# Rotary keys of four tiles at once, transposes inside projections, and a later start of the last query latents

## The chip, the cores and the metric

The kernel runs on one core of a Trainium2 chip. The metric is the device time of one execution in microseconds (us). TensorE, below also PE, does the matrix products and the transposes; VectorE (DVE), ScalarE (ACT) and GpSimd (POOL) do the rest, of which GpSimd works on SBUF alone; SP issues most DMAs.

## The reference

One layer of a bidirectional encoder for 1024 tokens and 16 learned meta tokens of width 1024, in float32. After an RMS norm one projection feeds two kinds of attention: multi-head latent attention (8 heads, queries and keys rebuilt from latents of 256) and neighbourhood attention (16 heads on a grid of 16 by 64 tokens). Each result is multiplied with a SiLU gate; an output projection and the residual follow. The part that matters here:

```python
q_nope, q_pe = split(rmsnorm(q_lat) @ w_uq)        # 128 + 64 per head
k_nope, v    = split(rmsnorm(kv_lat) @ w_ukv)      # 128 + 128 per head
q = [rmsnorm(q_nope), rope(rmsnorm(q_pe))]         # positions 0 to 1039
k = [rmsnorm(k_nope), rope(rmsnorm(k_pe))]         # k_pe: one rotary key for all heads
o = softmax(q k^T / sqrt(192)) v
```

## The kernel before

Products of float32 are made of three matmuls on rounded parts, high times high, low times high and high times low; so a value that TensorE will read is evicted twice, a high part (often by ScalarE) and a low part, the difference (often by VectorE: `lo_of`, L114). Weights are loaded into `wnf` and split by casts into `wnh` (L160) and `wnl`.

The stages are: gates, the neighbourhood attention (a pipelined loop over `g`, whose last six steps fill TensorE with projections of key-value latents), the rest of the latents, the latent attention (a loop over steps `s`, head `h` and query tile `t` of 128 rows, eight tiles a head), and the output projection. On TensorE the instructions stand in the order in which the code issues them, and it runs them in that order. On the other engines a scheduler puts them in order by its own estimate of time, and each engine then keeps that order.

The latents: there are eight tiles of 128 tokens and a ninth, number 8 (`NT`), of the 16 meta tokens. For each, `proj` makes the key-value latent and the raw rotary key (320 columns, 24 matmuls, for the meta tile 16), `lat_nat` takes squares on ScalarE, makes the inverse root mean square (`rstd`, a chain of small instructions with a power on GpSimd) and scales (`natl`), `lat_rope` rotates the key of a tile, and `lat_tr` transposes latent and key and evicts them (`klT`, `KH`, `KL`). `order` is the order of these tiles. Then come the same for the q latents (256 columns, `qlT`), and among them head 0's key-value tiles: `kv_tile` (6 matmuls of 256 columns, normalization of the keys, values into `mV`) and two steps later `kv_tr` (transposes into `mkT`). `q_tile` makes a query tile of a head pair (6 matmuls of 384 columns, `mqraw`, `mqr` the rotated part) and two steps later `q_tr` transposes it into `mq`.

In a step of the latent attention TensorE does the scores of the tile in three blocks of columns (`m_qk`, 348, 346 and 346 columns, 5 matmuls each), and with them the transposes of the probabilities of the step before (`m_ptr`), the products with the values (`m_pv`), and the tiles of the next head by the list `kv_now` and `q_now`. What a step has put into `pend` is transposed two steps later. In before, head 0's query tile `s+4` is made in step `s`, transposed in step `s+2` and used in step `s+4`.

Of the kernel before, what the change touches and what calls it, by code (L numbers as in the profile page):

```python
# [49 lines left out]
def hybrid_layer(ctx, tc, x, x_t, meta, meta_t, norm_w, w_na, w_g, w_lat, lat_w, w_uq, w_ukv, vec128, qpe_w, kpe_w,  # L50
# [634 lines left out]
    def lat_nat(t, acc, q, sq, pieces=None, late=None):

        n = P if t < NT else NM
        k = 1 if q else 2
# [13 lines left out]
        if pieces:  # L702
            nats[q, t] = pieces
            for k_, pc in enumerate(pieces):
                V.tensor_scalar(pc, acc[:, k_ * P:(k_ + 1) * P], r[:, 0:1], None, op0=ALU.mult)
            return
# [165 lines left out]
    def lat_rope(t):  # L872
        n = P if t < NT else NM
        kr = mk.tile([P, P], F32, name="kr", tag="mkn", bufs=6)[:n]
        rope(kr.rearrange("p (h k d) -> p h k d", h=1, k=2), nats.pop(("pe", t)).rearrange("p (h d) -> p h d", h=1),
             tabk[:n, t], n, 1, mk, V)
        nats["r", t] = kr

    def lat_tr(t, q, bank):
        n = P if t < NT else NM  # L880
        kc = k0 = slice(t * P, t * P + n)
        ps = bank("tr").rearrange("p (k n) -> p k n", k=4)[:, :, :n]
        nat = nats.pop((q, t))
        for k in range(2):
            tr(ps[:, k, :], nat[k])
        if not q:
            tr(ps[:, 2, :], nats.pop(("r", t)))
# [22 lines left out]
    for t in order[:3]:  # L910
        lat_rope(t)
    for i in range(LEAD, NT + 1):
        t = order[i]
# [3 lines left out]
        for k in ((0, 1), (2, 3, 4), (5, 6))[i - LEAD]:
            lat_tr(order[k], False, bank)
        for k in ((3, 4), (5, 6), (7,))[i - LEAD]:
            lat_rope(order[k])  # L920
    lat_rope(order[NT])
# [41 lines left out]
    for i in range(NT):  # L963
        acc = bank("o" if i % 2 else "s")[:, :256]
        proj(acc, i, wq, 0, 256)
        lat_nat(i, acc, True, lat_sq(), None if i < NT - 1 else
                [mk.tile([P, P], F32, name="natq", tag="mkn", bufs=6) for _ in range(2)])
# [6 lines left out]
        if i < 2:  # L974
            lat_tr(order[NT - 1 + i], False, bank)
        else:
            lat_tr(i - 2, True, bank)
        for ts_ in (((), (), (0, 1), (2, 3), (4,), (5,), (6,), (7, 8))[i],):
# [383 lines left out]
```

## Time and profile before

| | |
|---|---|
| median of 3 runs | 1341.32 us (1341.28 to 1343.41) |
| profiled execution | 1344.79 us, span 1343.0 us |
| granted TensorE clock over the span | 0.992 |
| latents, from the end of the neighbourhood attention | 672.75 to 739.79 us |
| latent attention, head 0 (eight steps) | 739.79 to 794.76 us |
| heads 1 to 7 | from 794.76 us, to about 1150 |

A step's start is the first matmul of its scores (`mps_s<-mkT,mq`, 348 columns). In a timeline an instruction stands with start, duration and, in brackets, the idle time of its engine ahead of it and what ended it. Consecutive matmuls overlap in the timeline, so the distance of two starts tells the pace and not the duration.

### The profile page before, as it was taken

To read this page: it belongs to the slowest core of one execution; us is meant where nothing else is said; L and a number is where in the kernel's file an instruction comes from. 1 tells how busy PE (TensorE), PEld (TensorE's weight loads), DVE (VectorE), ACT (ScalarE), POOL (GpSimd) and SP (SyncE) were. 2 spreads that over 40 slices of the span, in tenths; PEclk is the share of its full clock that TensorE was granted. 3 is DMA by queue.
4 is the path that set the end of the run, shared out by engine and by line. 5 is a ranking of instruction groups with operands and counts; after the bars stand their busy time and mean duration, and the time that the engine had idled before them with its cause. 6 is when DMAs were issued, how large, how long until landed. Compare 5 with 4: busy or idle time off the path is not lost.

```text
span 1343.0 us, 24641 instructions
## 1 busy us (share of the span) xinstructions
PE 1301.1 (97%) x8116; PEld 1202.7 (90%) x8116; DVE 956.9 (71%) x3100; ACT 806.5 (60%) x2263; POOL 398.2 (30%) x851
## 2 busy tenths in 40 slices
PE   9999999999999999999987999999999999999999
PEld 7888889999999999998987989999999999988887
DVE  4933236898988988888778889988988998542110
ACT  6622135787777878777755767777777786531010
POOL 4422102212122112212345437526625751000000
PEclk9999999999999999999999999999999999999999
DMA  9352640131212222111121010000100122353231
GB/s 340 134 175 82 213 140 27 52 102 49 76 42 79 79 70 71 45 57 51 44 60 52 13 37 23 33 27 24 34 32 17 48 80 75 87 173 118 81 96 47
DMA packets 82254, 103.59 MB, mean 77 GB/s; under 512 B 10311, under 2 KB 60871, under 8 KB 82007
## 3 DMA queue, kind: packets, MB, share of 16 engines
q1 hardware_dynamic: 82127, 102.02, 24.2%
q8 instruction: 64, 1.05, 0.3%
q14 instruction: 63, 0.52, 0.1%
HBM read 70.80 MB, written 24.90 MB: 71 GB/s over the span
## 4 chain that ended last, share of the span: by engine, by line
PE 61%; DVE 20%; ACT 11%; issue 4%; DMA 2%; POOL 1%; SPq 0%; ACTq 0%; DVEq 0%; POOLq 0%
PE ps_acc L117 14%; PE mps_acc L117 10%; PE mps_s L117 8%; PE ps_s L117 8%; PE mps_st L117 7%; PE mps_o L117 5%; PE mps_tr L120 4%; PE ps_o L117 3%; ACT s_sb L592 2%; DVE qs L557 2%; ACT qz L554 2%; PE ps_tr L120 2%; DVE s_sb L587 2%; DVE PT L114 2%; DVE m_sb L1034 2%
## 5 line engine op out<-in xcount | busy, mean ns | idle before, releaser
L93 POOL TENSOR_TENSOR rs_y<-rs_v,mhalf 128x1 f32<-128x1 f32 (+5 forms) x170 | 149.4, 882 | 84.0 <-DVE rs_v L89 61.3
L117 PE MATMUL ps_acc<-wnh,hT 128*128 128x384 f32 (+1 forms) x432 | 159.5, 369 | 0.0
L117 PE MATMUL ps_acc<-wnh,hTl 128*128 128x384 f32 (+1 forms) x432 | 144.6, 335 | 0.0
L117 PE MATMUL ps_acc<-wnl,hT 128*128 128x384 f32 (+1 forms) x432 | 144.1, 334 | 0.0
L558 POOL CAST qs<-qz 64x128 fp32r<-64x128 f32 x128 | 38.3, 299 | 339.5 <-ACT qz L554 327.1
L117 PE MATMUL mps_s<-mkT,mq 128*128 128x346 f32 (+1 forms) x576 | 132.3, 338 | 1.3 <-DVE mPT L114 0.9
L1060 ACT CAST mPT<-mps_tr 128x512 fp32r<-128x512 f32 x128 | 74.4, 583 | 54.5 <-PE mps_tr L120 53.4
L117 PE MATMUL mps_o<-mPT,mV 128*128 128x256 f32 x768 | 106.2, 287 | 0.0
L1034 DVE TENSOR_SCALAR_CACHE_REDUCE m_sb<-mps_s 128x346 f32<-128x346 f32 (+1 forms) x192 | 97.4, 513 | 10.0 <-PE mps_s L117 8.0
L592 ACT ACTIVATE s_sb<-s_sb,nmn 128x400 f32<-128x400 f32 (+1 forms) x128 | 76.7, 600 | 38.7 <-DVE nmn L587 38.3
L114 DVE TENSOR_TENSOR mPT<-mps_tr,mPT 128x512 fp32r<-128x512 f32 x128 | 87.7, 686 | 13.4 <-ACT mPT L1060 12.2
L117 PEld LDWEIGHTS mps_s<-mkT,mq 128*128 128x128 f32 x576 | 93.4, 192 | 3.2 <-DVE mPT L114 1.5
L117 PEld LDWEIGHTS mps_o<-mPT,mV 128*128 128x128 f32 x768 | 94.8, 189 | 0.2
L1043 ACT ACTIVATE m_sb<-m_sb,mnm 128x1040 f32<-128x1040 f32 x64 | 74.7, 1166 | 20.8 <-DVE mnm L1042 14.8
L117 PEld LDWEIGHTS ps_acc<-wnh,hT 128*128 128x128 f32 x432 | 81.4, 189 | 0.9
L117 PEld LDWEIGHTS ps_acc<-wnl,hT 128*128 128x128 f32 x432 | 81.9, 190 | 0.0
L117 PEld LDWEIGHTS ps_acc<-wnh,hTl 128*128 128x128 f32 x432 | 81.1, 188 | 0.0
L612 ACT CAST PT<-ps_tr 128x384 fp32r<-128x384 f32 (+2 forms) x160 | 62.7, 414 | 28.5 <-PE ps_tr L120 27.4
L120 PE MATMUL mps_tr<-ident,m_sb 128*128 128x128 f32 x512 | 76.7, 273 | 2.6 <-DVE mq L114 1.0
L114 DVE TENSOR_TENSOR PT<-ps_tr,PT 128x384 fp32r<-128x384 f32 (+2 forms) x160 | 72.3, 468 | 2.0 <-ACT PT L612 0.5
L114 POOL TENSOR_TENSOR wnl<-wnf,wnh 128x384 fp32r<-128x384 f32 (+2 forms) x62 | 52.4, 865 | 60.5 <-ACT wnh L160 53.4
L120 PEld LDWEIGHTS mps_tr<-ident,m_sb 128*128 128x128 f32 x512 | 60.9, 140 | 5.6 <-ACT wnh L160 1.3
(477 smaller groups left out, 3917.8 us busy)
## 6 DMA issues: line engine op xcount, KB each, us to landing
wnf<-in_w_na_dram SPq DMA_DIRECT2D x32, 384.0 KB, 3.5
g_d<-g SPq DMA_DIRECT2D x32, 256.0 KB, 2.5
wnf<-in_w_out_dram SPq DMA_DIRECT2D x32, 256.0 KB, 2.8
wnf<-in_w_g_dram SPq DMA_DIRECT2D x19, 384.0 KB, 5.7
Vp<-Vt SPq DMA_DIRECT2D x48, 112.0 KB, 2.2
yfo<-y_d SPq DMA_DIRECT2D x24, 192.0 KB, 2.8
gt<-g_d SPq DMA_DIRECT2D x16, 256.0 KB, 3.9
y_d<-y_na SPq DMA_DIRECT2D x16, 256.0 KB, 3.6
```

Source lines behind the costliest of these rows:

```text
L93: G.tensor_tensor(y, v, mhalf[:np_, :n], op=ALU.pow)
L114: eng.tensor_tensor(dst, src, f(hi), op=ALU.subtract)
L117: T.matmul(o, lhsT=l, rhs=r, start=start, stop=stop, skip_group_check=True)
L120: T.transpose(out=o, in_=i, identity=ident[: i.shape[0], : i.shape[0]])
L554: lambda: [S.activation(qz[i, j], ps[i, :P], AF.Copy, scale=qkwn[i]) for j, i in enumerate((slice(0, 64), slice(64, P)))])
L557: V.scalar_tensor_tensor(qs[l_, j], ps[l_, :P], qkwn[l_], f(qz[l_, j]), op0=ALU.mult, op1=ALU.subtract)
L558: G.tensor_copy(qs[h_, j], qz[l_, j])
L592: S.activation(sb, sb, AF.Exp, scale=-1.0, bias=mn, accum_out=d["sum", t // 4][:, t % 4, j:j + 1])
L612: S.copy(pt[:n, c0:c1, 0, :], ps[:n, c0:c1])
L1034: V.tensor_scalar(st["sb", h, t][:, ks], s_ps, -SCALE, BIG, op0=ALU.mult, op1=ALU.min, accum_out=st["mx", h, t][:, b:b + 1])
L1043: S.activation(sb, sb, AF.Exp, scale=-1.0, bias=nm, accum_out=st["ms", h, t // 2][:, t % 2:t % 2 + 1])
L1060: S.copy(dh, ps)
```

## The change

- `order` is 0, 1, 2, 3, meta, 4 to 7: the meta tile moves from the first place to the fifth. Its sum of parts, squares and scaling are written out in `lat_nat`.
- The raw rotary keys go into one tile `pe9`, and `lat_rope` rotates the meta tile, four tiles and four tiles in three calls. `lat_kr` transposes the keys of four tiles into one bank and evicts them at once.
- `lat_tr` handles two tiles, and its transposes stand in the middle of a projection (matmuls 0 to 4 and 4 to 8 of `proj`).
- The scale of the q latents is made on GpSimd (before on VectorE apart from the power) and applied by ScalarE (before by VectorE).
- The q weights are loaded ahead of the first key-value weights, and head 0's key-value tiles come one projection later.
- The last two q latents are transposed in step 0 of the attention, query tile 3 is made there, and tile 2 transposed there. In head 0 tile `s+3` is made in step `s`.
- The key-value tiles of the next head are made at other steps.

```diff
-    order = [NT] + list(range(NT))
+    pe9 = hp.tile([P, NT + 1, 64], F32, name="pe9")
+    order = [0, 1, 2, 3, NT, 4, 5, 6, 7]
...
-        r = rstd(ss, k, 1.0 / 256 if q else cnt[:, :k], n, V if q else G)
+        r = rstd(ss, k, 1.0 / 256 if q else cnt[:, :k], n, G)
...
-        V.tensor_scalar(nat[:, :256], acc[:, :256], r[:, 0:1], None, op0=ALU.mult)
-        nats[q, t] = [nat[:, k_ * P:(k_ + 1) * P] for k_ in range(2)]
+        if not pieces:
+            S.activation(nat, acc, AF.Copy, scale=r[:, 0:1])
+            pieces = [nat[:, k_ * P:(k_ + 1) * P] for k_ in range(2)]
+        else:
+            for k_, pc in enumerate(pieces):
+                S.activation(pc, acc[:, k_ * P:(k_ + 1) * P], AF.Copy, scale=r[:, 0:1])
+        nats[q, t] = pieces
...
+    def lat_rope(t0, t1):
+        n, m = P if t0 < NT else NM, t1 - t0
+        tmp = krt[:n, t0 * 64:t1 * 64].rearrange("p (t k d) -> p t k d", k=2, d=32)
+        pe = pe9[:n, t0:t1].rearrange("p t (k d) -> p t k d", d=32)
+        tab = tabk[:n, t0:t1]
+        V.tensor_tensor(tmp[:, :, 0:1], pe[:, :, 1:2], tab[:, :, 2:3], op=ALU.mult)
+        V.tensor_tensor(tmp[:, :, 1:2], pe[:, :, 0:1], tab[:, :, 3:4], op=ALU.mult)
+        V.tensor_tensor(pe, pe, tab[:, :, 0:2], op=ALU.mult)
+        dst = krm[:n] if t0 == NT else kr8[:, t0:t1]
+        two = lambda a: a.rearrange("p t k d -> p t (k d)")[:, :, None, :].to_broadcast([n, m, 2, 64])
+        V.tensor_tensor(dst, two(pe), two(tmp), op=ALU.add)
+    def lat_kr(t0, t1, bank):
+        n = P if t0 < NT else NM
+        ps = bank("tr")
+        w = 0
+        for t in range(t0, t1):
+            src = krm[:n, 0] if t == NT else kr8[:, t]
+            tr(ps[:, w:w + n], src.rearrange("p k d -> p (k d)"))
+            w += n
+        kc = slice(t0 * P, t0 * P + w)
+        S.copy(KH[:, kc], ps[:, :w])
+        lo_of(KL[:, kc], ps[:, :w], KH[:, kc])
...
+    wq = w_load(lambda k: w_lat[:, 2 * k:2 * k + 2, 0:256], 256, (V, V))
     kv_load(0)
-    kv_alloc(0)
-    wq = w_load(lambda k: w_lat[:, 2 * k:2 * k + 2, 0:256], 256, (V, V))
     q_load(0)
     kv_load(1)
...
     for i in range(NT):
-        acc = bank("o" if i % 2 else "s")[:, :256]
-        proj(acc, i, wq, 0, 256)
-        lat_nat(i, acc, True, lat_sq(), None if i < NT - 1 else
+        acc = bank("o")[:, :256]
+        proj(acc, i, wq, 0, 256, 0, 4)
+        if i == 0:
+            lat_tr(4, 6, False, bank)
+        if i in (2, 4, 6):
+            lat_tr(i - 2, i, True, bank)
+        if i >= 7:
+            q_tr(0, i - 7, bank)
+        proj(acc, i, wq, 0, 256, 4, 8)
+        lat_nat(i, acc, True, lat_sq(), None if i < NT - 2 else
                 [mk.tile([P, P], F32, name="natq", tag="mkn", bufs=6) for _ in range(2)])
...
-        for t in ((8, 0), (1, 2), (3, 4), (5, 6), (7,), (), (), ())[i]:
+        for t in ((8,), (0, 1), (2, 3), (4, 5), (6, 7), (), (), ())[i]:
             kv_tile(0, t, bank)
...
-        if i >= 6:
-            q_tr(0, i - 6, bank)
-    for t in range(2, LQ):
-        q_tr(0, t, bank)
+    q_tr(0, 1, bank)
...
-        lat_tr(NT - 2, True, mbank)
-        q_tile(0, LQ, mbank, m2, *QE0)
-        pend = [([], []), ([], [(0, LQ)])]
+        pend = [([], [(0, LQ - 1)]), ([], [])]
...
-                kv_now = [(h + 1, k) for k in ((), (0,), (1, 2), (3, 4), (5, 6), (7, 8), (), ())[t]]
+                kv_now = [(h + 1, k) for k in ((), (0,), (1,), (2,), (3, 4), (5, 6), (7, 8), ())[t]]
...
-            if s + LQ + 1 < NT:
-                q_now = [(0, s + LQ + 1)]
+            if s + LQ < NT:
+                q_now = [(0, s + LQ)]
...
-                lat_tr(NT - 1, True, mbank)
+                lat_tr(NT - 2, NT, True, mbank)
```

The first place is the end of step 2 of head 0 on TensorE. `mqraw` and `mqr` are the query tile that is transposed, `mps_acc` a key-value tile, `PS` and `mr` small transposes of the step, and the last rows are the first scores of step 3. Before:

```order
L120 MATMUL mps_tr_9950<-ident_62,mqraw_9743 128x128 x2
L120 MATMUL mps_tr_9950<-ident_62,mqr_9761 128x128
L117 MATMUL mps_acc_9961<-wnh_8650,klT0_8585 128x256
L117 MATMUL mps_acc_9961<-wnl_8651,klT0_8585 128x256
...
L117 MATMUL mps_acc_9984<-wnh_8650,klT0_8585 128x256
...
L120 MATMUL mps_tr_10007<-ident_62,PS0_9691 64x128
L120 MATMUL mps_tr_10007<-ident_62,mr_9817 128x128 x2
L117 MATMUL mps_s_10035<-mkT0_8609,mq_9870 128x348
L117 MATMUL mps_s_10035<-mkT1_8610,mq_9870 128x348
```

And in the changed kernel:

```order
L120 MATMUL mps_tr_9826<-ident_62,mqraw_9619 128x128 x2
L120 MATMUL mps_tr_9826<-ident_62,mqr_9637 128x128
L117 MATMUL mps_acc_9837<-wnh_8649,klT0_8588 128x256
L117 MATMUL mps_acc_9837<-wnl_8650,klT0_8588 128x256
...
L120 MATMUL mps_tr_9860<-ident_62,PS0_9565 64x128
L120 MATMUL mps_tr_9860<-ident_62,mr_9704 128x128 x2
L117 MATMUL mps_s_9888<-mkT0_8656,mq_9830 128x348
L117 MATMUL mps_s_9888<-mkT1_8657,mq_9830 128x348
```

Before, the scores read `mq_9870`, which comes from transposes of step 1 (`mps_tr_9866`); `mps_tr_9950` is for step 4. In the changed kernel they read `mq_9830`, which is evicted from `mps_tr_9826`, the transposes at the top of these rows, and one key-value tile stands between in place of two.

The second place is step 0 of head 2 on TensorE, behind the transposes of a query tile of the next pair: the first scores read head 2's keys. Before:

```order
L120 MATMUL mps_tr_11654<-ident_62,mqraw_11403 128x128 x2
L120 MATMUL mps_tr_11654<-ident_62,mqr_11422 128x128
L117 MATMUL mps_s_11671<-mkT0_10579,mq_10896 128x348
...
L117 MATMUL mps_s_11671<-KL_8592,mq_10896 128x348
L117 MATMUL mps_s_11678<-mkT0_10579,mq_10896 128x346
...
L117 MATMUL mps_s_11678<-KL_8592,mq_10896 128x346
L117 MATMUL mps_s_11685<-mkT0_10579,mq_10896 128x346
L117 MATMUL mps_s_11685<-mkT1_10580,mq_10896 128x346
```

And in the changed kernel:

```order
L120 MATMUL mps_tr_11573<-ident_62,mqraw_11274 128x128 x2
L120 MATMUL mps_tr_11573<-ident_62,mqr_11293 128x128
L117 MATMUL mps_s_11590<-mkT0_10495,mq_10817 128x348
...
L117 MATMUL mps_s_11590<-KL_8595,mq_10817 128x348
L120 MATMUL mps_tr_11597<-ident_62,mkn_11326 128x128
L120 MATMUL mps_tr_11597<-ident_62,mkn_11362 128x16
L117 MATMUL mps_s_11602<-mkT0_10495,mq_10817 128x346
...
L117 MATMUL mps_s_11602<-KL_8595,mq_10817 128x346
L117 MATMUL mps_s_11609<-mkT0_10495,mq_10817 128x346
```

The transposes of the last two key tiles (`mkn`, one of 128 and one of 16 rows) of head 2 now stand behind the first block of its scores. They stood in step 6 of head 1.

## Rows read from the trace of the kernel before

**Rows 1.** Page, part 1: busy time of each engine, share of the span, instructions.

```profile
PE 1301.1 (97%) x8116; PEld 1202.7 (90%) x8116; DVE 956.9 (71%) x3100; ACT 806.5 (60%) x2263; POOL 398.2 (30%) x851
```

**Rows 2.** Windows: stretch, length, each engine's busy time, granted clock, DMA share, GB/s.

```profile
672.75:739.79 67.04, 55.44 (x402) 53.08 (x400) 54.37 (x243) 36.21 (x139) 33.95 (x76) 0.92 0.20 58
744.62:794.76 50.14, 46.48 (x327) 43.99 (x327) 46.18 (x194) 36.08 (x106) 22.56 (x46) 0.97 0.08 25
795.00:1150.00 355.00, 348.80 (x2602) 341.21 (x2601) 309.44 (x1164) 263.67 (x739) 175.03 (x439) 1.00 0.13 40
672.75:676.44 3.69, 3.69 (x27) 3.50 (x24) 2.46 (x5) 1.74 (x5) 2.51 (x10) 1.00 0.02 4
679.00:688.00 9.00, 8.67 (x60) 8.03 (x59) 7.15 (x38) 4.85 (x21) 3.15 (x11) 1.00 0.21 67
694.50:697.80 3.30, 3.30 (x18) 3.30 (x17) 3.16 (x12) 1.80 (x8) 1.60 (x2) 0.51 0.52 153
737.40:742.20 4.80, 4.79 (x17) 4.80 (x18) 1.71 (x7) 1.63 (x4) 0.00 (x0) 0.50 0.34 105
783.30:786.60 3.30, 3.30 (x14) 3.24 (x14) 2.31 (x10) 1.49 (x7) 0.73 (x2) 0.51 0.00 0
```

**Rows 3.** Timeline of PE, latents: start, duration, line, operation, shapes [idle <-releaser].

```profile
637.14 0.70 PE L117 MATMUL ps_s<-kM,qz 128*128 128x400 f32 x1 [2.81 <-DVE kM L114]
...
678.61 0.23 PE L120 MATMUL ps_tr<-ident,kr 16*128 16x16 f32 x1 [1.87 <-DVE kr L371]
...
692.87 0.39 PE L117 MATMUL ps_s<-wnh,hT 128*128 128x256 f32 x1 [1.77 <-ACT wnh L160]
...
730.33 0.41 PE L120 MATMUL ps_tr<-ident,mqraw 128*128 128x128 f32 x2 [1.88 <-DVE natl L709]
731.80 0.41 PE L120 MATMUL ps_tr<-ident,mqraw 128*128 128x128 f32 x2 [0.96 <-DVE mq L114]
733.36 0.47 PE L120 MATMUL ps_tr<-ident,mqr 128*128 128x128 f32 x1 [1.15 <-DVE mqr L371]
...
737.41 0.66 PE L120 MATMUL mps_tr<-ident,natl 128*128 128x128 f32 x2 [3.58 <-DVE mq L114]
```

**Rows 4.** Timeline of ScalarE, one weight cast, before the first wait.

```profile
634.25 0.62 ACT L160 CAST wnh<-wnf 128x512 fp32r<-128x512 f32 x1 [1.15 <-DMA wnf<-in_w_lat_dram]
```

**Rows 5.** Timelines of ScalarE, GpSimd: from squares to scale of one latent tile.

```profile
676.61 0.38 ACT L695 ACTIVATE sql<-ps_s 128x256 f32<-128x256 f32 x1 [2.04 <-POOL cq L806]
...
677.51 0.21 POOL L91 TENSOR_TENSOR rs_v<-ssl,cnt 128x2 f32<-128x2 f32 x1 [0.69 <-ACT sql L697]
...
680.08 0.23 POOL L106 TENSOR_TENSOR rs_y<-rs_y,rs_t 128x2 f32<-128x2 f32 x1
```

**Rows 6.** PE and VectorE, head 0: a query tile's transposes, last low part.

```profile
754.26 0.38 PE L120 MATMUL mps_tr<-ident,mqraw 128*128 128x128 f32 x2
...
756.25 0.72 PE L117 MATMUL mps_s<-mkT,mq 128*128 128x348 f32 x3
...
758.96 0.59 DVE L114 TENSOR_TENSOR mq<-mps_tr,mq 64x128 fp32r<-64x128 f32 x2
```

**Rows 7.** Timeline of PE, head 0: its three longest waits.

```profile
777.82 0.63 PE L120 MATMUL mps_tr<-ident,m_sb 128*128 128x128 f32 x4 [1.02 <-DVE mq L114]
...
781.20 0.41 PE L120 MATMUL mps_tr<-ident,mqraw 128*128 128x128 f32 x2 [0.91 <-DVE mqraw L938]
782.64 0.33 PE L120 MATMUL mps_tr<-ident,mqr 128*128 128x128 f32 x1 [1.02 <-POOL mqr L371]
```

**Rows 8.** Timelines: key pieces' transposes on PE, low part evicted.

```profile
783.78 0.63 PE L120 MATMUL mps_tr<-ident,mkn 128*128 128x128 f32 x2
...
784.85 0.42 DVE L114 TENSOR_TENSOR mkT<-mps_tr,mkT 128x256 fp32r<-128x256 f32 x1
```

**Rows 9.** Timeline of PE: double key-value tiles of odd heads.

```profile
870.71 0.39 PE L117 MATMUL mps_acc<-wnh,klT 128*128 128x256 f32 x1 [1.07 <-DVE mV L114]
...
1084.78 0.38 PE L117 MATMUL mps_acc<-wnh,klT 128*128 128x256 f32 x1 [1.26 <-DVE mV L114]
```

More of the change, by code (lines that the diff above doesn't have):

```diff
@@ L690, in lat_nat @@
         if not pieces:
-            nat = hp.tile([P, 320], F32, name="natl", bufs=6)[:n]
+            nat = hp.tile([P, 256], F32, name="natl", bufs=6)[:n]
         if t == NT:
-            meta_sum(nat, acc)
-            acc = nat
+            S.copy(nat, acc[32:MW, :256])
+            V.tensor_tensor(nat, acc[:NM, :256], nat, op=ALU.add)
+            pm = pe9[:n, t]
+            S.copy(pm, acc[32:MW, 256:])
+            V.tensor_tensor(pm, acc[:NM, 256:], pm, op=ALU.add)
+            S.activation(sq[:n], nat, AF.Square, accum_out=ss[:, 0:1])
+            S.activation(sq[:n, :64], pm, AF.Square, accum_out=ss[:, 1:2])
+            r = rstd(ss, k, cnt[:, :k], n, G)
+            V.tensor_scalar(nat, nat, r[:, 0:1], None, op0=ALU.mult)
+            V.tensor_scalar(pm, pm, r[:, 1:2], None, op0=ALU.mult)
+            nats[False, t] = [nat[:, k_ * P:(k_ + 1) * P] for k_ in range(2)]
+            return
         S.activation(sq[:n], acc[:, :256], AF.Square, accum_out=ss[:, 0:1])
@@ L701, in lat_nat @@
             return
[L702 to L706, printed above, removed]
         if not q:
             return lat_nat2(t, acc, nat, r)
-        V.tensor_scalar(nat[:, :256], acc[:, :256], r[:, 0:1], None, op0=ALU.mult)
-        nats[q, t] = [nat[:, k_ * P:(k_ + 1) * P] for k_ in range(2)]
+        if not pieces:
[5 more added lines that the diff above has]
+        nats[q, t] = pieces
     LEAD = 6
@@ L870, in kv_tr, with lat_tr @@
         lo_of(kT[1][:, kc], ps[:, :w], kT[0][:, kc])
[L872 to L887, printed above, removed]
+    def lat_rope(t0, t1):
[20 more added lines that the diff above has]
+        lo_of(KL[:, kc], ps[:, :w], KH[:, kc])
+    def lat_tr(t0, t1, q, bank):
+        n = P if t0 < NT else NM
+        m = (t1 - t0) * n
+        kc = slice(t0 * P, t0 * P + m)
+        ps = bank("tr").rearrange("p (k n) -> p k n", k=2)[:, :, :m]
+        for t in range(t0, t1):
+            nat = nats.pop((q, t))
+            for k in range(2):
+                tr(ps[:, k, (t - t0) * n:(t - t0 + 1) * n], nat[k])
         dst = qlT if q else klT
-        if t == NT:
+        if t0 == NT:
             dst, kc = (kmT[:, :, :NM], kmT[:, :, 32:]), slice(0, NM)
@@ L893, in lat_tr @@
             S.activation(dst[0][:, k, kc], ps[:, k, :], AF.Copy, scale=w[k])
-        if not q:
-            S.copy(KH[:, k0], ps[:, 2, :])
         for k in range(2):
@@ L898, in lat_tr @@
                                    op0=ALU.mult, op1=ALU.subtract)
-        if not q:
-            lo_of(KL[:, k0], ps[:, 2, :], KH[:, k0])
     def lat_sq():
         return mk.tile([P, 2 * P], F32, name="sql", tag="msq", bufs=1)
+    wq = w_load(lambda k: w_lat[:, 2 * k:2 * k + 2, 0:256], 256, (V, V))
     kv_load(0)
-    kv_alloc(0)
-    wq = w_load(lambda k: w_lat[:, 2 * k:2 * k + 2, 0:256], 256, (V, V))
     q_load(0)
     kv_load(1)
-    for t in order[:3]:
-        lat_rope(t)
+    kr8 = mk.tile([P, L], F32, name="kr8", tag="mkT0")[:, :D].rearrange("p (t k d) -> p t k d", k=2, d=64)
+    krt = mk.tile([P, L], F32, name="krt", tag="mkT1")
+    krm = krt[:, 768:896].rearrange("p (t k d) -> p t k d", k=2, d=64)
+    kv_alloc(0)
+    lat_rope(NT, NT + 1)
+    lat_rope(0, 4)
     for i in range(LEAD, NT + 1):
         t = order[i]
-        acc = bank("acc" if i % 2 else "s")[:, :320]
-        proj(acc, t, wk, 0, 320)
-        lat_nat(t, acc, False, lat_sq())
[L917 to L921, printed above, removed]
+        acc = bank("o" if i % 2 else "acc")[:, :320]
+        proj(acc, t, wk, 0, 320, 0, 4)
+        if i == LEAD + 1:
+            lat_tr(0, 2, False, bank)
+        if i == LEAD + 2:
+            lat_kr(0, 4, bank)
+        proj(acc, t, wk, 0, 320, 4, 8)
+        lat_nat(t, acc, False, lat_sq())
+        if i == LEAD + 1:
+            lat_tr(NT, NT + 1, False, bank)
+            lat_kr(NT, NT + 1, bank)
+        if i == LEAD + 2:
+            lat_tr(2, 4, False, bank)
     def q_tile(hp_, t, bank, m2, E=G, EA=None, ER=G):
@@ L963, in hybrid_layer @@
     for i in range(NT):
-        acc = bank("o" if i % 2 else "s")[:, :256]
-        proj(acc, i, wq, 0, 256)
-        lat_nat(i, acc, True, lat_sq(), None if i < NT - 1 else
+        acc = bank("o")[:, :256]
[8 more added lines that the diff above has]
+        lat_nat(i, acc, True, lat_sq(), None if i < NT - 2 else
                 [mk.tile([P, P], F32, name="natq", tag="mkn", bufs=6) for _ in range(2)])
+        if i == 0:
+            lat_rope(4, 8)
+        if i == 1:
+            lat_tr(6, 8, False, bank)
         if i == 3:
+            lat_kr(4, 8, bank)
             h0ctx.close()
@@ L971, in hybrid_layer @@
             lq = hctx.enter_context(tc.tile_pool(name="latq", bufs=1, reuse_waits="tile"))
-        for t in ((8, 0), (1, 2), (3, 4), (5, 6), (7,), (), (), ())[i]:
+        for t in ((8,), (0, 1), (2, 3), (4, 5), (6, 7), (), (), ())[i]:
             kv_tile(0, t, bank)
[L974 to L978, printed above, removed]
+        for ts_ in ((), (), (0, 1), (), (2, 3), (4, 5), (6, 7, 8), ())[i:i + 1]:
             if ts_:
```

5 lines of the change are left out of this document (3 added, 2 removed).

## The prediction

> **What bounds the kernel now.** I read the busy times first: TensorE is busy 1301.1 of the 1343.0 us span, VectorE 956.9 [rows 1]. So the kernel is TensorE's work plus the places where TensorE stands still, and the second view is a table of stretches that looks for those. The heads 1 to 7 of the latent attention hold few: 348.80 of 355.00 us. The latents stretch holds many, 55.44 of 67.04 us, and head 0 behind it 46.48 of 50.14, where VectorE is busy nearly as long, 46.18 [rows 2]. Together these two stretches have 15.3 us in which TensorE does nothing, and they are what the change rewrites. The third view is TensorE's timeline there, where each wait names its releaser: 1.87 us for a rotated key, 1.77 us for a weight cast, and at the end 1.88, 0.96, 1.15 and 3.58 us, all in the short chain that takes the first query tiles into the attention [rows 3]. [...]
>
> The profiled execution took 1344.79 us, its span 1343.0 with 1.8 around it, and lies 3.47 above the median of 1341.32. I add up the change of the span and put it on the median.
>
> **Part 1, the order of the key-value tiles.** The meta tile has 16 matmuls of the 24 of an ordinary tile. It was the first of the six that fill the end of the neighbourhood attention, and a hole of 2.81 us stood behind it [rows 3]. An ordinary tile takes 3.69 us for its 24 matmuls (beside them stand the ends of three earlier transposes) [rows 2], 0.15 each, so eight more lay 1.2 us of work over that hole and take the same 1.2 us off a later step that has none. Bounds: nothing, if the hole's cause (ScalarE's cast, which stood until its weights landed [rows 4]) moves back by as much, and -3.6 if that hole and a smaller one close. I take **-1.2**.
>
> **Part 2, the latents.** Removed: the two waits of 1.87 and 1.77 (the rotations come in batches ahead of their transposes; the q weights are asked for before the key-value ones), and the four at the end, 7.57 together, because two q latents and one query tile leave this chain: 11.2 us [rows 3]. Of the two spells at half clock I leave one, so 2.4 more go. TensorE's own work only moves: some 1.7 us of it now stands in the first attention step.
>
> Added: the scale of a q latent is now worked out on GpSimd, in seven instructions, and applied by ScalarE. For a key-value latent the same chain took from 676.61 (first square) to 680.31 (last GpSimd instruction), 3.70 us [rows 5]; with one more ScalarE instruction of about 0.5 (an estimate from the 0.38 of the square of the same shape) that is 4.2. The transposes of tiles 0 and 1 now stand in the middle of tile 2's projection. Of work between tile 1's last matmul and them there is half a projection (an estimate of 1.4 us: twelve matmuls of 256 columns, at four fifths of the 0.15 that 320 take), and the key-value tiles and transposes around it, 3.3 us at most. With nothing queued the wait is 0.9, with the weight casts in front on ScalarE up to 4; I take 2.6. For tiles 2 and 3 I take 0.5, for 4 and 5 1.8, by the same count. In front of the first scores half a projection and one pair of transposes cover 1.8 of the 3.58 that this very chain took before, 1.8 stay. The last two q latents are transposed in step 0, behind 2.4 us of scores; their ScalarE copies stand in line behind casts that wait for weights, as the cast of 634.25 did [rows 4]: 2.0. Small ones 0.4. Sum 9.1 us, bounds 5 and 13. Part 2 is -11.2 - 2.4 + 9.1 = **-4.5**, bounds -8.6 and -0.6.
>
> The batched rotations (three calls of four VectorE instructions for nine) I cost at nothing: they save VectorE time that is covered by projections. The wide evictions, four tiles' keys in one, likewise: the next reader of them is the attention.
>
> **Part 3, head 0.** This is where I expect the loss. Before, a query tile's transposes came two steps ahead of its scores. Now query tile 3 is made only in step 0, and tiles 3 to 7 are transposed at the end of steps 2 to 6, straight in front of the scores that need them. What lies between is one key-value tile and three small transposes in step 2 (some 1.0 us), three small transposes in steps 4 and 6 (0.3 each), nothing in steps 3 and 5. Behind the waiting scores stand that step's key-value tile and the transposes of the step before, so ScalarE's and VectorE's next evictions wait with them. The latency from transposes to the last low part was 754.26 to 759.55, 5.3 us, in a loaded queue [rows 6], and 3.58 where TensorE already stood [rows 3]. The shortest it can be is one ScalarE eviction, one on VectorE and two small low parts, some 2.0 with their hand-overs (0.59 for the last two [rows 6]). Five times 3.58 less 1.6 of cover is 16.3; five times 2.0 less 1.6 is 8.4. While TensorE waits, the other queues empty, so I take a value between them, 11.0. What goes are waits that came because VectorE had fallen behind, 1.02, 0.91 and 1.02 [rows 7]; the spell at half clock at their end stays [rows 2]. Part 3 is 11.0 - 2.95 = **+8.0**. From below it is bounded by 0: VectorE has 46 us of work in 50, and if that sets the pace anyway TensorE's new waits take the place of old ones. From above by 13.4, and more if the clock falls each time.
>
> **Part 4, the head boundaries.** In heads 1 to 7 key-value tiles come one step later and single in step 2, so the last two of a head are transposed in step 0 of the head that reads them, between its first and second block of scores. The third block needs them. Before, transposes at 783.78 had their low part done at 785.27, 1.5 us later [rows 8]; the second block and the transposes cover about 1.0. So each of seven boundaries waits 0.5 at least, and the three at which a query tile's evictions and a weight cast stand in front on ScalarE and VectorE about 1 more: some 4.7 together. Against it, the second tile of step 2 waited for the first one's low part in three odd heads, 1.07 and 1.26 in the first and last of them [rows 9], some 3.1 together, and that goes. Part 4 is **+1.6**, bounds -2 and +6.
>
> **Sum.** -1.2 - 4.5 + 8.0 + 1.6 = +3.9; on the median of 1341.3 that is 1345.2 us. The forecast is a little slower, its own range 1343 to 1350. A change of under 0.2% (2.7 us) can't be told from none here.
>
> **Rivals.**
> A, faster: VectorE paces head 0. The row for it is 46.18 of 50.14 us there [rows 2]. Then the transposes that come late cost nothing, part 3 is 0, and with the waits of part 2 at their lower end (5 for 9.1) and part 4 at 0 the sum is -1.2 - 8.6 + 0 = -9.8, 1331.5; with part 2 as taken, -5.7, 1335.6. I put the case at 1334. Against it: VectorE can't fill its time when the scores that it evicts come late, and a chain from TensorE over two engines and back is a latency, not work. It decides if the five waits sum to under 5 us.
>
> B, no change: the chain behind a transpose is at its shortest, 8.4 in the five, so part 3 is +5.5 and part 4 at 0: -0.2, 1341.1. For it: the steps of head 0 leave ScalarE 14 us of 50 idle [rows 2].
>
> C, much slower: each late transpose also drops the clock. After the wait of 1.77 us TensorE ran 3.30 us at 0.51, and after the waits up to 782.64 another 3.30 at 0.51 [rows 2, 3, 7]. Four spells more at 1.65 us are 6.6: 1351.8. Against it, after the 1.87 us of 678.61 the clock was 1.00 from 679 to 688 [rows 2, 3]: a wait of this size doesn't always drop it.
> [...]
>
> **How the numbers follow.** Forecast 0.38, A 0.27, B 0.20, C 0.15. Faster is A and a sliver of B, 0.28; the same is the rest of B and the lower edge of the forecast's range, 0.22; slower 0.50. The range leaves out the far half of A and the upper half of C's spread: 1332 to 1354.
>
> **What the profile after would show.** Right, if TensorE's timeline has five waits of 1.5 to 3.5 us in front of the first scores of steps 3 to 7 of head 0, released by a query tile's eviction; if the stretch from the first latent projection to the second attention step has shrunk by some 4 to 6 us with waits inside the projections on q latents scaled by ScalarE; and if the third block of scores at the start of heads 1 to 7 waits for key pieces while the waits in the odd heads' step 2 are gone. Wrong, if head 0 keeps its 50 us, which is A, or if granted clock in it falls well below 0.97, which is C. The sum also fails if the evictions of the transposes go ahead of the others in their queues, or if weights that are asked for in a new order land later than before.

## Result and profile after

The changed kernel takes 1362.62 us (median of 4 runs, 1361.09 to 1364.06), the kernel before in the same runs 1342.37: the ratio is 1.015, interval 1.0136 to 1.0164. It is slower, as forecast, but by 20 us where 4 were forecast, and it lies above the forecast's own range (1343 to 1350) and above the whole spread (1332 to 1354). The profiled execution took 1363.58 us, its span 1361.5.

TensorE's instructions are the same in number, 8116, and its busy time has grown by 8.6 us over the 1301.1 of before [rows 1]; VectorE has less to do than before. First the busy times after:

```profile
PE 1309.7 (96%) x8116; PEld 1206.3 (89%) x8116; DVE 949.8 (70%) x3019; ACT 808.5 (59%) x2257; POOL 405.6 (30%) x891
```

To see where the span's 18.5 us went, I cut it at three marks, each the `KH` matmul of a step's first block of scores: step 1 of head 0, step 0 of head 1 and step 1 of head 7. They stand at 745.09, 795.32 and 1121.18 us before, at 736.63, 802.93 and 1139.35 after. So the latents stretch with all ahead of it gained 8.5 us, head 0 lost 16.1, heads 1 to 7 lost 10.6, and the rest 0.3. The table of stretches, between these marks, before (columns as in rows 2, the busy time of TensorE first, the granted clock third from the end):

```profile
745.09:795.32 50.23, 46.57 (x328) 44.09 (x327) 45.79 (x193) 36.17 (x108) 22.61 (x47) 0.97 0.08 25
795.32:1121.18 325.86, 320.36 (x2399) 313.67 (x2398) 285.61 (x1092) 243.01 (x689) 171.79 (x431) 1.00 0.11 36
```

And after:

```profile
736.63:802.93 66.30, 54.16 (x332) 50.31 (x331) 51.70 (x209) 37.79 (x110) 24.03 (x48) 0.87 0.07 25
802.93:1139.35 336.42, 323.70 (x2401) 313.71 (x2400) 288.43 (x1098) 243.24 (x696) 172.18 (x431) 1.00 0.11 35
```

In head 0 TensorE stood still for 12.1 us (66.30 less 54.16) where it was 3.7, and it was busy 7.6 us longer at a mean clock of 0.87 for 0.97. In heads 1 to 7 the clock is full in both; there it stood still for 12.7 us in place of 5.5, and the remaining 3.3 are busy time. TensorE's timeline after, the hole of part 1 and the long waits from there up to the first scores:

```profile
636.87 0.45 PE L117 MATMUL ps_s<-kM,qz 128*128 128x400 f32 x1 [1.49 <-DVE kM L114]
...
696.76 0.44 PE L120 MATMUL ps_tr<-ident,natl 128*128 128x128 f32 x2 [2.90 <-ACT natl L717]
...
722.07 0.44 PE L120 MATMUL ps_tr<-ident,natl 128*128 128x128 f32 x2 [1.91 <-ACT natl L717]
...
729.84 0.71 PE L117 MATMUL mps_s<-mkT,mq 128*128 128x348 f32 x3 [1.80 <-DVE mq L114]
```

Against [rows 3] the waits for a rotated key, for a weight cast and the four at the end are gone, and three new ones have come, two of them for q latents scaled by ScalarE (`natl`, L717). Then head 0, all waits for `mq`, the query tiles:

```profile
750.50 0.43 PE L117 MATMUL mps_s<-mkT,mq 128*128 128x348 f32 x1 [2.57 <-DVE mq L992]
...
759.75 0.58 PE L117 MATMUL mps_s<-mkT,mq 128*128 128x348 f32 x2 [0.73 <-ACT mq L987]
...
761.20 0.43 PE L117 MATMUL mps_s<-mkT,mq 128*128 128x348 f32 x1 [0.87 <-DVE mq L992]
...
771.95 0.58 PE L117 MATMUL mps_s<-mkT,mq 128*128 128x348 f32 x2 [1.08 <-ACT mq L987]
...
773.84 0.43 PE L117 MATMUL mps_s<-mkT,mq 128*128 128x348 f32 x1 [1.31 <-DVE mq L992]
...
782.90 0.94 PE L117 MATMUL mps_s<-mkT,mq 128*128 128x348 f32 x2 [2.43 <-ACT mq L987]
...
784.25 0.66 PE L117 MATMUL mps_s<-mkT,mq 128*128 128x348 f32 x1 [0.41 <-DVE mq L992]
...
794.58 0.58 PE L117 MATMUL mps_s<-mkT,mq 128*128 128x348 f32 x2 [1.23 <-ACT mq L987]
...
796.26 0.66 PE L117 MATMUL mps_s<-mkT,mq 128*128 128x348 f32 x1 [1.10 <-DVE mq L992]
```

These are the five places of the forecast, the first scores of steps 3 to 7, the later ones in two waits each, for the high part on ScalarE (L987) and the low one on VectorE (L992). The five come to 2.57, 1.60, 2.39, 2.84 and 2.33 us, 11.7 together. The stretch right behind each of the five, in the table of stretches:

```profile
751.00:754.30 3.30, 3.30 (x17) 3.30 (x18) 3.14 (x15) 1.05 (x6) 2.70 (x7) 0.62 0.00 0
761.20:764.50 3.30, 3.30 (x14) 3.17 (x15) 2.20 (x11) 0.90 (x5) 1.02 (x1) 0.63 0.00 0
773.90:777.20 3.30, 3.30 (x23) 3.17 (x24) 2.50 (x13) 1.13 (x7) 1.02 (x1) 1.00 0.27 84
784.30:789.50 5.20, 5.20 (x22) 4.92 (x22) 2.93 (x13) 1.16 (x6) 0.54 (x1) 0.52 0.00 0
796.30:799.60 3.30, 3.30 (x12) 3.21 (x13) 2.20 (x8) 0.37 (x1) 0.00 (x0) 0.50 0.13 43
```

The clock is down behind four of the five. In heads 1 to 7 the waits stand at the end of an odd head and at the start of the next one; here are those around the start of head 2 (862.88), and the one of head 3:

```profile
856.58 0.75 PE L117 MATMUL mps_s<-mkT,mq 128*128 128x346 f32 x3 [1.23 <-DVE m_sb L1076]
...
858.68 0.63 PE L120 MATMUL mps_tr<-ident,m_sb 128*128 128x128 f32 x4 [1.04 <-DVE mq L114]
...
865.28 0.43 PE L117 MATMUL mps_s<-mkT,mq 128*128 128x346 f32 x1 [0.65 <-ACT mkT L881]
...
866.28 0.59 PE L117 MATMUL mps_s<-mkT,mq 128*128 128x346 f32 x2 [0.58 <-DVE mkT L114]
...
914.36 0.58 PE L117 MATMUL mps_s<-mkT,mq 128*128 128x346 f32 x2 [0.36 <-DVE mkT L114]
```

Around the starts of heads 4 and 6 the same rows return with 0.45 to 1.24 us, and at the start of head 7 the transposes of the meta tile's keys wait 1.11 us (1133.75). The waits of [rows 9] are gone. (Before, those stood in step 2 of heads 2, 4 and 6, at 870.71, 976.79 and 1084.78: even heads, and not odd ones as the prediction has it.)

### The profile page after: what moved, and what is told of

It reads as the page before. It is cut to its first block, busy times and chain, and to the rows that moved or that the text cites. A ratio compares the mean times of both kernels' runs of the same rounds, so it can differ in the third digit from the quotient of the medians.

```text
span 1361.5 us, 24604 instructions
## 1 busy us (share of the span) xinstructions
PE 1309.7 (96%) x8116; PEld 1206.3 (89%) x8116; DVE 949.8 (70%) x3019; ACT 808.5 (59%) x2257; POOL 405.6 (30%) x891
## 4 chain that ended last, share of the span: by engine, by line
PE 60%; DVE 17%; ACT 14%; issue 4%; DMA 3%; POOL 2%; SPq 0%; ACTq 0%; POOLq 0%; DVEq 0%
PE ps_acc L117 13%; PE mps_acc L117 10%; PE ps_s L117 8%; PE mps_s L117 7%; PE mps_st L117 7%; PE mps_o L117 5%; PE mps_tr L120 4%; PE ps_o L117 4%; ACT s_sb L592 3%; DVE qs L557 2%; ACT qz L554 2%; DVE PT L114 2%; PE ps_tr L120 2%; DVE s_sb L587 2%; DVE kM L114 1%
## 5 line engine op out<-in xcount | busy, mean ns | idle before, releaser
L117 PE MATMUL mps_s<-mkT,mq 128*128 128x346 f32 (+1 forms) x576 | 139.0, 347 | 21.7 <-DVE mq L992 6.2
```

The source lines that it names most:

```text
L117: T.matmul(o, lhsT=l, rhs=r, start=start, stop=stop, skip_group_check=True)
```

## Experiments

Each time is the median of the run's executions, and each ratio is to the kernel before on the same chip.

**Query tiles two steps ahead again.**

```diff
     q_tr(0, 1, bank)
+    q_tr(0, 2, bank)
...
-        pend = [([], [(0, LQ - 1)]), ([], [])]
+        q_tile(0, LQ, mbank, m2, *QE0)
+        pend = [([], []), ([], [(0, LQ)])]
...
-            if s + LQ < NT:
-                q_now = [(0, s + LQ)]
+            if s + LQ + 1 < NT:
+                q_now = [(0, s + LQ + 1)]
```

> The changed kernel (1362.6 us), but head 0's query tiles run two steps ahead of their scores again: tile 2 is transposed and tile 3 made before the first scores, tile s+4 is made in step s. Theory one (late transposes, and the clock that falls behind each of their waits, made head 0 16.1 us longer): steps 1 to 7 go back from 66.3 to 50 to 52 us, so 1347 to 1349 us. Rival (VectorE paces head 0 and the new waits only stand in for its backlog): the waits of 11.7 us move to other places, and it gains 5 us at most, 1358 or more.

Measured 1350.30 us, ratio 1.0053 (1.0038 to 1.0068), so 12.3 under the changed kernel and 1.3 above the range that theory one gave. Head 0 fell further than I expected, to 46.1 us at full clock, and the latents stretch gave 3.5 us back: step 1 begins at 740.18 for 736.63, with a wait for a q latent on ScalarE in step 0. Stretch and wait:

```profile
740.18:786.27 46.09, 43.80 (x326) 42.26 (x325) 42.74 (x189) 34.77 (x104) 21.72 (x43) 1.00 0.09 27
```

```profile
733.85 1.23 PE L117 MATMUL mps_s<-mkT,mq 128*128 128x346 f32 x3 [3.77 <-ACT natq L721]
```

Theory one holds, and the rival, that the waits only stand in for VectorE's backlog, falls: VectorE is busy 42.7 us of 46.1 there and the five waits are gone; TensorE stands still for 2.3 us there in all.

**Filling the waits with useless work.**

```diff
+            if 2 <= s <= 6:
+                fb = mbank("tr")
+                for _ in range(16):
+                    mm(fb[:, :256], klT[0][:, 0, :P], klT[0][:, 1, :256], True, True)
             pend.append((kv_now, q_now))
```

> The changed kernel with 16 matmuls of 256 columns more at the end of each of steps 2 to 6 of head 0, into a bank that nothing reads, so that TensorE works while it waits for the query tile (about 1.9 us at full clock in waits of 1.5 to 2.8). Nothing is left out. If half of head 0's loss is the clock that falls behind the waits (granted 0.87 there, 0.97 before): the clock goes back to 0.95 or more and head 0 shortens by 5 to 7 us, 1356 to 1358, though 80 matmuls were added. If the clock falls anyway, or costs nothing beside the waits: 1363 to 1368.

Measured 1356.22 us, ratio 1.0094 (1.0079 to 1.0109): 80 matmuls more and 6.4 us less than the changed kernel. The table of stretches for head 0, and TensorE's waits in it:

```profile
735.80:794.36 58.56, 55.69 (x412) 53.10 (x411) 50.04 (x209) 37.97 (x109) 24.10 (x48) 1.00 0.09 29
```

```profile
749.70 0.43 PE L117 MATMUL mps_s<-mkT,mq 128*128 128x348 f32 x1 [0.64 <-DVE mq L992]
...
769.91 0.43 PE L117 MATMUL mps_s<-mkT,mq 128*128 128x348 f32 x1 [0.73 <-DVE mq L992]
...
789.03 0.43 PE L117 MATMUL mps_s<-mkT,mq 128*128 128x348 f32 x1 [1.03 <-DVE mq L992]
```

The clock is 1.00, the stretch 58.6 us for 66.3. (Heads 1 to 7 then take 1.7 more: they hold a spell of 3.3 us at clock 0.50, from 960.1, that the changed kernel does not have.) So about half of head 0's loss, 7.7 of 16.1 us, was the clock that fell behind the waits, and the rest the waits themselves.

**The old list of key-value steps.**

```diff
-                kv_now = [(h + 1, k) for k in ((), (0,), (1,), (2,), (3, 4), (5, 6), (7, 8), ())[t]]
+                kv_now = [(h + 1, k) for k in ((), (0,), (1, 2), (3, 4), (5, 6), (7, 8), (), ())[t]]
```

> The changed kernel with the list of steps at which the next head's key-value tiles are made as it was before. Theory one (the list costs heads 1 to 7 10.6 us: key pieces that arrive in the step that reads them, and VectorE behind in the last step of odd heads): minus 10.6, 1352.0 us, and the waits of 1.23 and 1.04 us at the end of odd heads are gone. Rival (what I forecast for this part): only 1.6 us come back, 1361.0, and the rest of the heads' loss has another cause, such as the clock.

Measured 1349.12 us, ratio 1.0049 (1.0032 to 1.0066): 13.5 less. Heads 1 to 7 take 325.8 us, as before the change, and head 0, too, is 3.9 shorter (62.4), at a mean clock of 0.92 for 0.87. The two stretches:

```profile
736.91:799.32 62.41, 51.97 (x335) 47.81 (x333) 50.13 (x209) 38.11 (x109) 24.35 (x48) 0.92 0.07 23
799.32:1125.14 325.82, 320.19 (x2398) 313.54 (x2398) 285.53 (x1091) 243.09 (x689) 171.74 (x430) 1.00 0.11 36
```

The rival, my term of 1.6, falls.

**The new list alone, in the kernel before.** The same line, the other way round.

> The kernel before with one line of the change alone, the new list of steps for the next head's key-value tiles. If that list is the whole cause of what heads 1 to 7 lost (336.4 for 325.9 us): plus 10.6, 1353.5 us, and heads 1 to 7 take 336 us. If the loss needs the rest of the change beside it: 1345 or less.

Measured 1352.79 us, ratio 1.0064 (1.005 to 1.0079), about 8.6 more than before. Heads 1 to 7 take 339.7 us (13.8 more, of which about 1.5 go to a spell at clock 0.50, from 845.6 to 848.9) and head 0 45.7 (4.5 less). Only two of head 0's 328 matmuls have moved out of it; TensorE stands still for 1.9 us in place of 3.7 there, and the clock is 1.00 for 0.97. The waits of the changed kernel are there without the rest of the change:

```profile
843.91 0.75 PE L117 MATMUL mps_s<-mkT,mq 128*128 128x346 f32 x3 [1.23 <-DVE m_sb L1034]
...
846.01 1.08 PE L120 MATMUL mps_tr<-ident,m_sb 128*128 128x128 f32 x4 [1.03 <-DVE mq L114]
...
855.14 0.58 PE L117 MATMUL mps_s<-mkT,mq 128*128 128x346 f32 x2 [1.50 <-DVE mkT L114]
```

The list needs nothing else to cost most of what it cost.

**The last pair of key-value tiles alone.** The kernel with both costs undone (below, under that name), and only tiles 7 and 8 moved, to step 6:

```diff
-... ((), (0,), (1, 2), (3, 4), (5, 6), (7, 8), (), ())[t]]
+... ((), (0,), (1, 2), (3, 4), (5, 6), (), (7, 8), ())[t]]
```

> The same starting point (1340.0 us), with only the last pair (7 and 8) moved from step 5 to step 6 and so its transposes into step 0 of the head that reads them; tiles 0 to 6 where they were before. If the last pair alone makes the loss in heads 1 to 7 (its normalization in VectorE's queue at the end of odd heads, its transposes in front of the scores): plus 10 to 14, for the waits of step 2 (3 us) stay as well, 1350 to 1354. If the other tiles' delay shares in it: 1343 to 1346.

Measured 1351.18 us, ratio 1.0054 (1.0038 to 1.0069); heads 1 to 7 take 337.9 us for 325.9 without that move:

```profile
788.42:1126.35 337.93, 326.74 (x2401) 316.84 (x2400) 285.23 (x1095) 244.58 (x692) 173.00 (x431) 0.99 0.11 35
```

The last pair alone makes a loss as large as the whole list, but not in the same places. The waits at the end of the odd heads are not there: no wait in step 7 of heads 1, 3 and 5 is longer than 0.25 us. In their place the waits for key pieces at the starts of heads 2, 4 and 6 are longer, 1.65, 1.46 and 1.43 us, and two spells of 3.3 us at clock 0.50 (from 851.9 and 1087.4), about 3.3 us lost together, stand in these heads, which the changed kernel does not have. At the start of head 2, TensorE and ScalarE:

```profile
850.09 0.42 PE L117 MATMUL mps_s<-mkT,mq 128*128 128x346 f32 x1 [1.65 <-ACT mkT L881]
...
851.75 2.86 PE L117 MATMUL mps_o<-mPT,mV 128*128 128x256 f32 x12
```

```profile
848.30 0.46 ACT L965 COPY mqraw<-mps_acc 128x384 f32<-128x384 f32 x1
848.66 0.83 ACT L160 CAST wnh<-wnf 128x768 fp32r<-128x768 f32 x1
849.40 0.47 ACT L987 ACTIVATE mq<-mps_tr,qkw 128x256 fp32r<-128x256 f32 x1
849.76 0.27 ACT L881 CAST mkT<-mps_tr 128x144 fp32r<-128x144 f32 x1
```

The high part of the key pieces (`mkT`) stands on ScalarE behind a query tile's copy, a weight cast and another query tile's eviction; TensorE waits 1.65 us, and the 12 products behind it take 2.86 us, which elsewhere take 1.66: behind this wait, too, the clock is down, at 0.50 from 851.9.

**The last pair transposed one step after it is made**, from that kernel.

```diff
+            if t == 6 and kv_now:
+                pend[0] = (kv_now, pend[0][1])
+                kv_now = []
             pend.append((kv_now, q_now))
```

> The last pair of key-value tiles made in step 6 as in the run that moved it alone (1351.2 us, heads 1 to 7 at 337.9), but transposed one step later in place of two, in step 7 of the head before the one that reads it, so that no scores wait for it. If the loss is at the head's boundary (key pieces arriving in the step that reads them): the heads go back to 326 to 328 us, 1340 to 1342. If it is that VectorE and ScalarE do the pair's normalization in the last two steps: the waits move into step 7 and the time stays at 1349 to 1352. In step 7 the transposes themselves may wait for the normalization, up to 1 us a head, which both allow.

Measured 1377.56 us, ratio 1.0257 (1.0233 to 1.0282): worse than either theory allowed. TensorE waits in step 7 of every head up to head 6 for the meta tile's keys: 3.0 us in head 0, 4.2 in the odd heads, 2.7 in heads 2 and 4 and 4.9 in head 6. The first two of heads 1 to 6:

```profile
851.52 0.23 PE L120 MATMUL mps_tr<-ident,mkn 16*128 16x16 f32 x1 [4.21 <-DVE mkn L868]
...
905.84 0.23 PE L120 MATMUL mps_tr<-ident,mkn 16*128 16x16 f32 x1 [2.68 <-DVE mkn L868]
```

From the last matmul that makes them (841.5) to their normalized rows (851.5) it takes 10.0 us, longer than the 7.9 of step 6. So this run doesn't separate the boundary from the queues; it shows that here a pair made in step 6 isn't ready for step 7.

**Both undone.** The first and third of these edits together.

> Both of these undone; what stays is the change in the latents stretch. If the two costs and the latents' gain (8.5 us at the second attention step) are independent: 1362.6 - 15 - 10.6 = 1337, 5 us under the kernel before. If the latents gain only because work was put off into head 0: 1342, the same as before.

Measured 1339.97 us, ratio 0.9978 (0.9968 to 0.9989): faster than the kernel before, by 3 us and not 5. From step 1 of head 0 to step 1 of head 7 it takes 374.7 us (before 376.1), so the heads give nothing back; the latents stretch keeps 3.5 of its 8.5 us, since step 0 again holds a query tile and a wait of 3.6 us for the last q latents. (The 3.5 is rough: in the five runs with this order of query tiles and this scale step 1 begins between 739.93 and 741.91. The last section says why.)

**The scale of the q latents on VectorE again**, from that kernel.

```diff
-        r = rstd(ss, k, 1.0 / 256 if q else cnt[:, :k], n, G)
+        r = rstd(ss, k, 1.0 / 256 if q else cnt[:, :k], n, V if q else G)
...
-            S.activation(nat, acc, AF.Copy, scale=r[:, 0:1])
+            V.tensor_scalar(nat, acc, r[:, 0:1], None, op0=ALU.mult)
...
-                S.activation(pc, acc[:, k_ * P:(k_ + 1) * P], AF.Copy, scale=r[:, 0:1])
+                V.tensor_scalar(pc, acc[:, k_ * P:(k_ + 1) * P], r[:, 0:1], None, op0=ALU.mult)
```

> The kernel with both costs undone (head 0's query tiles two steps ahead, key-value list as before; 1340.0 us), and besides the scale of the q latents on VectorE again in place of GpSimd and ScalarE. If the waits of 2.9 and 1.9 us inside the projections and of 3.6 us in step 0 are the longer chain (4.2 us by my sum for GpSimd and ScalarE, about 2.5 for VectorE): they shrink by 1.5 to 2 each, 1335 us. If they are ScalarE's or VectorE's queue and not the chain: 1339 to 1341.

Measured 1335.43 us, ratio 0.9934 (0.9921 to 0.9946). The sum came as expected, its parts only in one of three places, so the agreement is in part luck. TensorE's waits:

```profile
696.00 0.44 PE L120 MATMUL ps_tr<-ident,natl 128*128 128x128 f32 x2 [2.69 <-DVE rs_y L103]
...
720.22 0.44 PE L120 MATMUL ps_tr<-ident,natl 128*128 128x128 f32 x2 [0.50 <-DVE natl L717]
...
730.06 0.33 PE L120 MATMUL ps_tr<-ident,mqr 128*128 128x128 f32 x1 [3.66 <-DVE mqr L371]
```

The first is 2.69 for 2.9, the second 0.50 for 1.93, and the one in step 0 is gone, with a wait of 3.66 for a rotated query key in its place, ahead of the first scores. Another part of the gain is the clock: with both undone it is 0.50 from 734.5 to 741.2, and here only from 730.9 to 734.2.

**Tiles 2, 3 and 4 in one step**, from the same kernel.

```diff
-... ((), (0,), (1, 2), (3, 4), (5, 6), (7, 8), (), ())[t]]
+... ((), (0,), (1,), (2, 3, 4), (5, 6), (7, 8), (), ())[t]]
```

> The same starting point (1340.0 us), with the key-value tiles at steps 1, 2, 3, 4, 5 of a head as 0; 1; 2, 3 and 4; 5 and 6; 7 and 8. The second tile of step 2 goes, as in the change, but the last pair stays in step 5. If the waits of about 1 us in step 2 of the odd heads are worth what they show, minus 3: 1337. If step 3, which now has three tiles, gets a wait in their place: 1340 or more.

Measured 1337.55 us, ratio 0.9957 (0.9943 to 0.997). Heads 1 to 7 take 323.4 us for 325.9: the waits of [rows 9] are gone and little took their place (the longest new wait is 0.63 us, in step 7 of head 6). This is the part of the new list that was worth having.

**Both gains together**, on the kernel with both costs undone.

> The two gains over the kernel with both costs undone (1340.0 us) taken together: the scale of the q latents on VectorE (1335.4 alone) and the key-value tiles as 0; 1; 2, 3 and 4; 5 and 6; 7 and 8 (1337.6 alone). They lie in different stretches, the one in the latents, the other in heads 1 to 7. If they add: 1333, 0.7 to 0.8% under the kernel before. If the earlier end of the latents only shifts a wait into the heads: 1335 or more.

Measured 1332.62 us, ratio 0.9912 (0.9895 to 0.9929): the two add, and this is the fastest version.

## Why the prediction was wrong

*The direction* was right, for the reason given; the size was not, by two terms, parts 3 and 4; parts 1 and 2 together were off the other way and hid 2.8 us of it.

*Parts 1 and 2* were forecast at -1.2 and -4.5 and came to -8.5 together at step 1. Of this, 1.1 us are there at the last wait of the neighbourhood attention (0.33, at 656.21 for 657.31), although eight matmuls more are executed by then; the 1.2 us that they take off a later step follow. So part 1 came to about -2.3. What it missed is a spell at half clock behind the old hole (0.50 from 636.7 to 639.9; after, the clock there is 1.00). Part 2 came to about -6.2. In it the waits inside the projections were 2.9 and 1.9 for my 2.6 and 1.8, and 1.8 before the first scores as forecast. The wait of 2.0 in step 0 doesn't show: between 730 and 739 us no wait is longer than 0.24, though one of 3.8 is there when query tiles run two steps ahead. From 657.31 to step 1 TensorE stood still for 11.6 us before, and for 7.3 after (from 656.21), where the waits of the forecast add up to 9.1. The stretch holds 526 matmuls for 540: eight fewer by part 1, and six fewer because one query tile is now made later. So a part of this gain was work and waiting put off into head 0. Of the two spells at half clock in the latents, 0.51 from 694.50 to 697.80 and 0.50 from 737.40 to 742.20 [rows 2], I left the first and took off the second, for 2.4, half of its 4.80 us; two of 3.3 us are left, from 697.2 and 731.4, at 0.50.

*Part 3* was forecast at +8.0 and came to +16.1. Its waits are 11.7 us for the 11.0 that I took, and the old ones of 2.95 went. The step that failed is "the spell at half clock at their end stays": I let head 0 keep one spell of 3.3 us, and it has four, one of them of 5.2 us in the table. That was rival C's mechanism, priced there at 6.6; the busy time that came on top is 7.6. I gave it 0.15, because after one of two waits of this size the clock had stayed; behind these it fell four times of five. (The argument was weaker than it looked: in the run with the new list alone, whose code up to there is that of the kernel before, the clock fell behind the other of these two waits, as the last section shows.) The fill experiment shows the clock as a cause of its own: with TensorE kept busy in the waits it stays at 1.00, and 6.4 us come back at the cost of 80 matmuls.

*Part 4* was forecast at +1.6, bounds -2 and +6, and came to +10.6. The 4.7 in it was added up wrongly: seven waits of 0.5 and three times about 1 more are 6.5, so part 4 should have been about +3.4 by its own terms. The waits that it priced came to 4.1 us at the starts of the heads (0.65, 0.58 and their like three times, 0.3 to 0.4 three times) and one of 1.11 at head 7, and the waits of [rows 9], 3.1, went. The step that failed is the count of what the moved tiles bring along: I priced the transposes in front of the scores and put nothing for the tiles' normalization on the other engines, which runs later with them. At the end of each odd head, where a query tile is also made in every step, TensorE now waits 1.23 and 1.04 us, 6.8 in three heads. VectorE's timeline after, in front of the first of them:

```profile
853.50 0.13 DVE L89 TENSOR_SCALAR rs_v<-mss 16x1 f32<-16x1 f32 x1
853.56 0.67 DVE L114 TENSOR_TENSOR mPT<-mps_tr,mPT 128x512 fp32r<-128x512 f32 x1
854.57 1.12 DVE L100 TENSOR_TENSOR rs_t<-rs_y 16x1 f32<-16x1 f32 x1 [0.34 <-POOL rs_y L93]
855.62 0.27 DVE L991 CAST mq<-mps_tr 64x128 fp32r<-64x128 f32 x1
...
856.01 0.50 DVE L1076 TENSOR_SCALAR_CACHE_REDUCE m_sb<-mps_s 128x348 f32<-128x348 f32 x1
```

VectorE has to pass the meta tile's inverse root (`rs_t<-rs_y`, 16 rows), which waits 0.34 us for GpSimd's power and then takes 1.12, before it evicts the scores of step 7 at 856.01, which TensorE waits for at 856.58. The list brings these waits by itself, for they are there in the kernel before with the new list alone (1.23 and 1.03). The last pair by itself does not: moved alone it makes a loss of 12.1 us (337.9 for 325.9) without them, by longer waits at the starts of the heads and two spells at half clock. Which of the other moved tiles brings the waits of step 7 is not shown. Nor is where the remaining 3.3 us of busy time come from; the run that was to separate boundary and queues doesn't do it. The new list costs 14.5 us beside late query tiles (402.7 for 388.2 us from step 1 to head 7) and 9.2 in the kernel before. The difference lies in head 0, where it costs 3.9 us in the one, with the mean clock at 0.87 for 0.92, and gives 4.5 back in the other, with 1.00 for 0.97; why the clock falls more often with it in the one is open.

*Rival A* (VectorE paces head 0) is refuted by its own sign: the five waits sum to 11.7 us, where it wanted under 5. The first experiment agrees: with the query tiles two steps ahead, head 0 goes from 66.3 to 46.1 us, less than the 50 that VectorE was to set. *Rival B* (the chain at its shortest) wanted 8.4 us in the five waits. Its 2.0 us for a chain was an estimate: in the trace of before the pieces are 0.48 (ScalarE, at 754.89), 0.48 (VectorE, at 758.39) and 0.59 us [rows 6], 1.55 together, and no row shows the hand-overs by themselves.

## What to carry to other kernels

Transposes that stand directly in front of the matmuls that read them cost a round trip over two engines each time, here a wait of 1.60 to 2.84 us in each of five steps; put a step's worth of other work between, even where the projections ahead get longer by it. Price such a wait with the clock behind it, above all where several come in a row, as the five did within 46 us, with the clock at 0.50 to 0.63 behind four of them. When a list moves an item by a step, move everything the item issues in your count, its normalization on the other engines too, and look at which step has no room for it. One trace tells the price of a spell at half clock, but not surely behind which wait it comes.

## What the runs showed of the hardware

The 1.12 us of VectorE's `rs_t<-rs_y` at 854.57 are far above what the instruction mostly takes: line 100 takes 0.16 us in the median of its 129 executions after. It multiplies two operands from SBUF, and while it ran GpSimd did the like (the tiles of all 851 instructions of GpSimd before are in SBUF [rows 1]). GpSimd's timeline at that time:

```profile
854.52 0.45 POOL L369 TENSOR_TENSOR mqraw<-mqraw,tabq 128x128 f32<-128x128 f32 x1
854.94 0.72 POOL L1138 TENSOR_TENSOR mgt<-mgt,mrp 128x256 f32<-128x256 f32 x1
```

In the odd head after it, at 964.21, the same instruction takes 1.11 us beside the same two of GpSimd; in both it ends with the second of them. In the run that moved the last pair alone, GpSimd has another order: only the first of the two (841.12, 0.45 us) stands beside the instruction, the next follows at 841.64, and the instruction takes 0.41:

```profile
841.17 0.41 DVE L100 TENSOR_TENSOR rs_t<-rs_y 16x1 f32<-16x1 f32 x1
```

Of the 129 executions after, 13 take longer than 0.3 us, 0.40 to 1.40, each beside an instruction of GpSimd with two operands, and 12 of them end within 0.04 us of the end of one such. GpSimd beside it is not enough: at 752.40 it takes 0.15 us with one of 0.47 beside it from 752.41. Where two instructions of GpSimd stand in a row, as here, it takes 1.11 to 1.40 us. That this is what makes TensorE wait in step 7 is not shown: the run that moved the last pair alone has neither the 1.12 us nor those waits, but it differs in more than GpSimd's order.

Whether the clock falls behind a wait is not told by the wait's length in these traces. In the kernel before, the clock is 1.00 behind the wait of 1.87 us at 678.61 and 0.51 behind the one of 1.77 at 692.87 [rows 2, 3]. With the new list alone, where the code up to there is the same, it is the other way round: 0.50 behind the wait of 1.87 us at 678.16 and 1.00 from 693.2 to 697.3, behind one of 1.79. The first of these in the table of stretches:

```profile
678.40:681.60 3.20, 3.20 (x13) 3.20 (x14) 1.65 (x15) 0.00 (x0) 1.13 (x5) 0.50 0.66 207
```

In the same way the clock is 0.50 for 3.3 us behind the wait of 2.90 us for a q latent at about 696.5 in the run with both costs undone and in the one with tiles 2, 3 and 4 in one step, and not in three others with the same code up to there (query tiles two steps ahead, the last pair alone, the last pair transposed a step later). Step 1 begins at 741.61 and 741.91 in the first two and between 739.93 and 740.23 in the three: one such spell, about 1.7 us (half of its 3.3), is what the same latents scatter by from one trace to the next.

Matmuls that compute nothing paid here: 80 of them in waits of 1.6 to 2.8 us kept the granted clock at 1.00 in place of 0.87 over head 0 and shortened the kernel by 6.4 us. The earlier transposes, with the query tiles two steps ahead, do the like: head 0 runs at 1.00 there too, with the five waits gone.
